# RWKV time mix: four products R k issued ahead of the triangular inversion, the bonus term issued behind the turned blocks

## The chip, the cores and the metric

The kernel runs on one core of a Trainium2 chip. A core has five engines that run their own instruction streams and meet at semaphores: TensorE (PE; its weight loads are listed as PEld), VectorE (DVE), ScalarE (ACT), GpSimd (POOL) and SyncE (SP, which issues transfers). The metric is the device time of one execution, in microseconds (us). Times come from the hardware: medians of timed runs, and one profiled execution whose trace gives every instruction's start and duration.

## The reference

The program is a stack of four layers (each a token mixer and a gated feed-forward block, FFN) on 256 tokens of width 1024, followed by two hybrid attention layers. Layers 0 and 3 mix tokens by RWKV-7. For each of 16 heads of 64 channels it runs, in float32:

```python
def step(state, inp):
    r_t, w_t, k_t, v_t, kk_t, a_t = inp
    sa = jnp.einsum('bhvk,bhk->bhv', state, kk_t)
    state = (state * w_t[:, :, None, :]
             - sa[..., None] * (kk_t * a_t)[:, :, None, :]
             + v_t[..., None] * k_t[:, :, None, :])
    return state, jnp.einsum('bhvk,bhk->bhv', state, r_t)
...
y = ((y - mu) * lax.rsqrt(var + RW_GN_EPS)).reshape(B, S, D) * ln_w + ln_b
y = y + (jnp.sum(rh * kh * r_k, axis=-1, keepdims=True) * vh).reshape(B, S, D)
out = (y * g).astype(h.dtype) @ w_out
```

The second line from the end is the bonus term: for each token and head the sum over channels of r·k·r_k, times the value row.

## The kernel before

Channels lie on partitions, two heads to a tile of 128, so R, K and their kin are eight tiles `c` of 128 x 256 tokens. The recurrence is done in two chunks of 128 tokens. `Rh[:, c]` and `KB[:, c]` hold the scaled r, and the scaled k beside the scaled kk·a. `amat` forms for each head a strictly triangular 128 x 128 matrix (`AKB`), which has to be inverted. The rest of the layer waits for this inversion, which has three parts:

- `inv_diag`: the 32 x 32 blocks on the diagonals of all heads are inverted together on DVE, by 31 steps of two instructions, `tmp` = A times X (L1316) and X += `tmp` (L1318). Each instruction reads what the one ahead of it wrote, so the 62 form one chain. The sizes run from 31 elements per partition up to 256 and down to 31 again.
- `inv_turn`: two DVE transposes of the result, `XN` (L1324) and `XT` (L1326).
- `inv_merge`: PE joins blocks of 32 to 64 and then to 128 (L1346, L1360, L1362, L1370, L1373), and ACT and DVE copy what it makes (L1348, L1351, L1354, L1364, L1366, L1387, L1389). ACT starts with L1351, a copy of `XN`.

Beside the inversion runs work that needs no inverse: for each `c`, `rmat` makes products of R with K and kk·a on PE (L1234), ACT copies them (L1240, into `ark` and over `KB[:, c]`) and POOL cuts triangles out of them (L906). `rmat` also makes `prod` = Rh·KB on DVE (L1237), which must be read before ACT writes over `KB[:, c]`; `rout` sums `prod` over channels on PE (L1246, into the PSUM bank `bo`), and multiplies the triangles with the values (L1252). After tiles 3 and 7, ACT copies the sums to `coef` (L1256). `gtc` is the output gate's product (L1215, L1218 on PE, L1220 on ACT), of which each call fills half. Then `bv` = (Vc + mu)·coef is built in four pieces by two DVE instructions each (L1269, L1271); it is first read in `rwkv_tail` (L1431). `rwkv_tail` holds all that needs the inverse; its first DVE instruction is L1432.

The order on each engine is not that of the source: a scheduler of the tile framework places each engine's instructions by its own estimate, within the dependences and within the buffers that the pools give. `prod` has two buffers, so the third product can't be written before PE has read the first, and so on. An engine executes its list strictly in order, so an instruction that waits holds back all that stand behind it. `tc.issue_after(ins)` keeps what it wraps behind `ins` in the scheduler's list.

Of the kernel before, what the change touches and what calls it, by code (L numbers as in the profile page):

```python
# [9 lines left out]
F32 = mybir.dt.float32  # L10
# [3 lines left out]
ALU = mybir.AluOpType  # L14
# [3 lines left out]
D, S, H, HD, DFF = 1024, 256, 16, 64, 2816  # L18
# [21 lines left out]
class Prog:  # L40
# [502 lines left out]
    def dsa(self, x, i):  # L543
        nc, tc = self.nc, self.tc
        xg, rf = self.prenorm(x, f"norm_mix{i}")
        with tc.tile_pool(name="ds", bufs=1) as sp, tc.tile_pool(name="dsw", bufs=2) as sw:
# [75 lines left out]
            def evac_qk(g, dst, sc):  # L622
                def ev(n, t, ps):
# [4 lines left out]
                    s8 = sw.tile([128, 8], F32, name="s8")  # L628
                    nc.vector.tensor_reduce(s8, sq.rearrange("p (h d) -> p h d", d=64), axis=AX.X, op=ALU.add)
                    rs = self.rstd(s8, scale=1.0 / HD, n=8, load=False)  # L630
# [264 lines left out]
    def rwkv(self, x, i):  # L895
        nc, tc = self.nc, self.tc
# [3 lines left out]
        mm, tt, ts, stt = nc.tensor.matmul, nc.vector.tensor_tensor, nc.vector.tensor_scalar, nc.vector.scalar_tensor_tensor  # L900
# [8 lines left out]
        with ExitStack() as outer:  # L909
# [11 lines left out]
            Vc = sp.tile([128, 2, D], F32, name="Vc")  # L921
# [4 lines left out]
            mu = sp.tile([128, 2, 16], F32, name="mu")  # L926
# [4 lines left out]
            coef = sp.tile([128, 2, 16], F32, name="coef")  # L931
            bcol = sp.tile([128, KT, 4], F32, name="bcol")
            with tc.tile_pool(name="ra", bufs=1) as ra:
# [76 lines left out]
                with tc.issue_after(xv_lo):  # L1010
                    for q, m in ((0, 3), (64, 4)):
                        tt(out=L1m[:, :, q:q + 64], in0=L1.rearrange("p (k n) -> p k n", n=128)[:, :, q:q + 64],
                        in1=C(f"mix{m}", 0, 8)[:, :, None].to_broadcast([128, 8, 64]), op=ALU.mult)
                def evac_v(n, t, ps):
# [16 lines left out]
                    m = mu[:, t, n * 8:n * 8 + 8]  # L1031
                    nc.vector.tensor_reduce(m, v3(v), axis=AX.X, op=ALU.add)
                    ts(m, m, 1.0 / HD, None, op0=ALU.mult)
# [38 lines left out]
            KB = rc.tile([128, KT, 2 * S], F32, name="KB")  # L1072
            Rh = rc.tile([128, KT, S], F32, name="Rh")
# [123 lines left out]
            with ExitStack() as rde:  # L1197
                rd = rde.enter_context(tc.tile_pool(name="rd", bufs=1))
                TT = [rd.tile([128, 16, 128], F32, name="TT0")]
                nc.gpsimd.memset(TT[0], 0.0)  # L1200
                X = self.inv_diag(rd, AKB)
                rt = rde.enter_context(tc.tile_pool(name="rt", bufs=1, side="right"))
                GT = rt.tile([128, KT, S], F32, name="GT")
                TT.append(rt.tile([128, 16, 128], F32, name="TT1"))
                act(TT[1], self.ones[:, None, :128].to_broadcast([128, 16, 128]), AF.Copy, scale=0.0)
                g2 = self.wraw.tile([128, WCH], F32, name="wraw")
                nc.sync.dma_start(g2[:, :1024], self.a["rw_g2a"][l])
                nc.sync.dma_start(g2[:, 1024:1280], self.a["rw_g2b"][l])

                def gtc(a):  # L1210

                    pg = [self.psum("at")[:, :S] for _ in range(4)]
                    for j in range(4):
                        c = 4 * a + j
                        mm(pg[j], g2[:, c * 128:128 + c * 128], sg1, start=True, stop=False)  # L1215
                    for j in range(4):
                        b = slice(32 * j, 32 * j + 32)
                        mm(pg[j], g2[b, 1024 + a * 128:1152 + a * 128], sg2[b], start=False, stop=True)  # L1218
                    for j in range(4):
                        cp(GT[:, 4 * a + j], pg[j])  # L1220
                rex = ExitStack()
                re = rex.enter_context(tc.tile_pool(name="re", bufs=2))
                bo = self.psum("o")
                ark = [re.tile([128, 4, 128], F32, name=f"ark{j}", bufs=1) for j in range(2)]
                prods = {}

                def rmat(c):
                    ak = ark[c % 2]
                    pe = [q4(self.psum("at")) for _ in range(2)]
                    for y in range(2):  # L1230
                        for ch in range(2):
                            for e in range(2):
                                b = slice(e * 64, e * 64 + 64)
                                mm(pe[e][:, 2 * y + ch], KB[b, c, y * S + ch * 128:y * S + ch * 128 + 128],  # L1234
                                   Rh[b, c, ch * 128:ch * 128 + 128], start=True, stop=True)
                    prods[c] = re.tile([128, S], F32, name="prod")
                    tt(out=prods[c], in0=Rh[:, c], in1=KB[:, c, :S], op=ALU.mult)  # L1237
                    for j, d in enumerate((ak, q4(KB[:, c]))):
                        for e in range(2):
                            cp(d[:, e::2], pe[e][:, 2 * j:2 * j + 2])  # L1240
                        lower(d, 0)

                def rout(c):
                    ak, prod = ark[c % 2], prods[c]
                    for t in range(2):
                        mm(bo[:, t * 16 + 2 * c:t * 16 + 2 * c + 2], prod[:, t * 128:(t + 1) * 128], rkb[:, c],  # L1246
                           start=True, stop=True)
                    py = self.psum("mm")[:, :S].rearrange("p (a b) -> p a b", b=64)
                    for ch in range(2):
                        for e in range(2):  # L1250
                            hh = 2 * c + e
                            mm(py[:, 2 * ch + e], ak[:, 2 * ch + e], Vc[:, ch, hh * 64:hh * 64 + 64], start=True, stop=True)  # L1252
                    cp(csT[:, c, :S], py.rearrange("p a b -> p (a b)"))
                    if c % 4 == 3:
                        o = slice(2 * c - 6, 2 * c + 2)
                        cp(coef[:, :, o], bo[:, :32].rearrange("p (a b) -> p a b", a=2)[:, :, o])  # L1256
                    prods[c] = None
                rph = [lambda: rmat(0)] + sum(([lambda c=c: rmat(c + 1), lambda c=c: rout(c)] if c + 1 < KT else [lambda c=c: rout(c)]
                                              for c in range(KT)), [])
                for j, f in enumerate(rph):  # L1260
                    f()
                    if j == 8:
                        gtc(0)
                rex.close()
                bv = rde.enter_context(tc.tile_pool(name="rv", bufs=1)).tile([128, 2, 4, 2, 2, 64], F32, name="bv")
                for q in range(2):
                    for ch in range(2):
                        bc = lambda u: u[:, ch, 8 * q:8 * q + 8].rearrange("p (c e) -> p c e", e=2)[:, :, :, None].to_broadcast([128, 4, 2, 64])
                        tt(out=bv[:, q, :, ch], in0=Vc[:, ch, 512 * q:512 * q + 512].rearrange("p (c e v) -> p c e v", e=2, v=64),  # L1269
                           in1=bc(mu), op=ALU.add)  # L1270
                        tt(out=bv[:, q, :, ch], in0=bv[:, q, :, ch], in1=bc(coef), op=ALU.mult)  # L1271
                scr = aT.rearrange("p c t -> p (c t)")
                XNT = self.inv_turn(rd, X)
                og, gts = [None] * KT, [lambda: gtc(1)]
                sc = [scr[:, 1024 * q:1024 * q + 1024] for q in range(2)]
                self.inv_merge([u.rearrange("p a h t -> p (a h) t") for u in AKB], XNT, TT, sc, lambda: gts and gts.pop()())

                def chain(q):
                    return self.rwkv_tail(q, rc, rt, l, Vc, AKB[q], KB, TT[q], csT, Rh, N0, W00, WK1, scol, bv[:, q], GT, sc[q], C, og)
                add = lambda c, ps: self.new_x(c, x[c], ps)  # L1280
                A, B, i, rest = chain(0), chain(1), 0, []
                while A or B:
                    if A and next(A, 1):
                        A = None
                        rest = self.ohalf(self.a["rw_out"][l], 0, og, add)
                    if B and i >= RLAG and next(B, 1):
                        B = None
                    for f in rest[:RFO]:
                        f()
                    rest = rest[RFO:]  # L1290
                    i += 1
                for f in rest + self.ohalf(self.a["rw_out"][l], 1, og, add):
                    f()
# [27 lines left out]
    def inv_turn(self, rd, X):  # L1321
        nc = self.nc
        XN = rd.tile([128, 32, 32], F32, name="XN_", tag="i1")
        nc.vector.transpose(XN, X.rearrange("p i j -> p j i"))  # L1324
        XT = rd.tile([128, 32, 32], F32, name="XT_", tag="i0")
        nc.vector.transpose(XT.rearrange("p a b -> p (a b)"), X.rearrange("p a b -> p (a b)"))  # L1326
        return XN, XT, rd.tile([128, 32, 32], F32, name="M1", tag="i2")

    def inv_merge(self, AKBs, XNT, TTs, scrs, turn):
# [369 lines left out]
```

## Time and profile before

| | |
|---|---|
| median of 3 runs | 1827.63 us (1822.09 to 1831.22) |
| profiled execution | 1820.38 us, of which the span of the trace is 1818.6 us |
| busy in the span | PE 95%, DVE 75%, ACT 56%, POOL 2% |
| mean granted PE clock | 0.963 of 2.4 GHz |
| `inv_diag`'s chain, first RWKV layer | first L1316 at 146.28 us, XN (L1324) at 185.19 us |
| the same, second RWKV layer | 1220.43 us and 1259.81 us |

Times within the trace count from the span's start. The profiled execution is 7.25 us (0.4%) below the median and 1.7 us below the fastest of the timed runs, so a sum made on the trace is made against 1820.38 us and then carried over to the median. A busy share is an average over stages; what a change is worth is read in its stage.

### The profile page before, as it was taken

To read this page: it belongs to the slowest core of one execution; us is meant where nothing else is said; L and a number is where in the kernel's file an instruction comes from. 1 tells how busy PE (TensorE), PEld (TensorE's weight loads), DVE (VectorE), ACT (ScalarE), POOL (GpSimd) and SP (SyncE) were. 2 spreads that over 40 slices of the span, in tenths; PEclk is the share of its full clock that TensorE was granted. 3 is DMA by queue.
4 is the path that set the end of the run, shared out by engine and by line. 5 is a ranking of instruction groups with operands and counts; after the bars stand their busy time and mean duration, and the time that the engine had idled before them with its cause. 6 is when DMAs were issued, how large, how long until landed. Compare 5 with 4: busy or idle time off the path is not lost.

```text
span 1818.6 us, 34203 instructions
## 1 busy us (share of the span) xinstructions
PE 1730.9 (95%) x13780; PEld 1571.9 (86%) x13780; DVE 1364.0 (75%) x2691; ACT 1021.4 (56%) x1851; POOL 36.4 (2%) x78
## 2 busy tenths in 40 slices
PE   7997899999999999999999989897999998999998
PEld 5696889999899999877999977786999997886876
DVE  8887499866688876799887669787686656676666
ACT  4965355555676455557645445764364445665664
POOL 0003000000000000000000000011000000000000
PEclk9997699999999999999999999986999999999999
DMA  6331048746427855633585542321155455433440
GB/s 218 111 108 47 14 169 302 249 162 225 162 96 280 290 191 176 234 124 116 202 312 207 175 155 101 121 86 44 31 214 187 162 185 206 163 140 124 175 161 24
DMA packets 53451, 293.23 MB, mean 161 GB/s; under 512 B 6651, under 2 KB 9739, under 8 KB 28588
## 3 DMA queue, kind: packets, MB, share of 16 engines
q1 hardware_dynamic: 49148, 285.66, 43.8%
q10 hardware_dynamic: 4144, 5.39, 0.9%
q8 instruction: 108, 1.77, 0.4%
q14 instruction: 51, 0.42, 0.1%
HBM read 288.92 MB, written 2.11 MB: 160 GB/s over the span
## 4 chain that ended last, share of the span: by engine, by line
PE 73%; DVE 14%; DMA 6%; ACT 4%; issue 3%; ACTq 0%; SPq 0%; DVEq 0%; POOLq 0%
PE mm L114 14%; PE mm L116 13%; PE mm L115 13%; PE mm L219 6%; PE mm L220 5%; PE mm L221 5%; DMA adaw<-ada 4%; DVE wlo L108 4%; DVE junk L675 1%; ACT whi L107 1%; PE o L508 1%; PE at L472 1%; PE at L1153 1%; PE at L1234 1%; PE at L495 1%
## 5 line engine op out<-in xcount | busy, mean ns | idle before, releaser
L108 DVE TENSOR_TENSOR wlo<-wraw,whi 128x1024 fp32r<-128x1024 f32 (+2 forms) x518 | 588.5, 1140 | 229.7 <-ACT whi L107 227.6
L107 ACT CAST whi<-wraw 128x1024 fp32r<-128x1024 f32 (+2 forms) x518 | 504.4, 983 | 312.2 <-PE mm L116 181.8
L1527 ACT ACTIVATE sg<-gt 128x256 f32<-128x256 f32 x88 | 36.8, 418 | 84.8 <-DVE gt L1524 84.7
L219 PE MATMUL mm<-whi,xgh 128*128 128x512 f32 x192 | 79.9, 419 | 3.3 <-ACT xgh L734 3.3
L220 PE MATMUL mm<-wlo,xgh 128*128 128x512 f32 x192 | 76.1, 397 | 0.1
L221 PE MATMUL mm<-whi,xgl 128*128 128x512 f32 x192 | 75.9, 398 | 0.0
L114 PE MATMUL mm<-mh,whi 128*128 128x256 f32 x256 | 73.9, 289 | 1.1 <-ACT sg L1062 0.6
L115 PE MATMUL mm<-mh,wlo 128*128 128x256 f32 x256 | 71.7, 280 | 0.0
L116 PE MATMUL mm<-ml,whi 128*128 128x256 f32 x256 | 71.6, 280 | 0.0
L1524 DVE TENSOR_TENSOR gt<-mm,rr 128x512 f32<-128x512 f32 x88 | 60.5, 688 | 12.7 <-PE mm L116 11.6
L675 DVE SCALAR_TENSOR_TENSOR junk<-adaw,cs 128x1024 f32<-128x1024 f32 x48 | 58.6, 1222 | 14.5 <-DMA adaw<-ada 14.1
L115 PE MATMUL mm<-xg0h,wlo 128*128 128x256 f32 x192 | 54.1, 282 | 4.6 <-DVE wlo L108 4.6
L114 PE MATMUL mm<-xg0h,whi 128*128 128x256 f32 x192 | 54.9, 286 | 0.8 <-ACT whi L107 0.8
L116 PE MATMUL mm<-xg7l,whi 128*128 128x256 f32 x192 | 53.5, 279 | 0.5 <-DVE xg7l L132 0.5
L114 PE MATMUL mm<-xg4h,whi 128*128 128x256 f32 x192 | 53.7, 280 | 0.0
L116 PE MATMUL mm<-xg0l,whi 128*128 128x256 f32 x192 | 53.3, 278 | 0.0
L114 PE MATMUL mm<-xg1h,whi 128*128 128x256 f32 x192 | 53.3, 278 | 0.0
L115 PE MATMUL mm<-xg1h,wlo 128*128 128x256 f32 x192 | 53.3, 277 | 0.0
L114 PE MATMUL mm<-xg5h,whi 128*128 128x256 f32 x192 | 53.3, 277 | 0.0
L116 PE MATMUL mm<-xg4l,whi 128*128 128x256 f32 x192 | 53.3, 277 | 0.0
L115 PE MATMUL mm<-xg5h,wlo 128*128 128x256 f32 x192 | 53.3, 277 | 0.0
L115 PE MATMUL mm<-xg4h,wlo 128*128 128x256 f32 x192 | 53.3, 277 | 0.0
(825 smaller groups left out, 6009.8 us busy)
## 6 DMA issues: line engine op xcount, KB each, us to landing
wraw<-ffn_gu SPq DMA_DIRECT2D x88, 1024.0 KB, 5.0
wraw<-ffn_dn SPq DMA_DIRECT2D x64, 704.0 KB, 4.0
adaw<-ada SPq DMA_DIRECT2D x48, 512.0 KB, 5.1
wraw<-hy_qkv SPq DMA_DIRECT2D x24, 1024.0 KB, 4.9
wraw<-rw_k SPq DMA_DIRECT2D x8, 1024.0 KB, 4.9
wraw<-rw_r SPq DMA_DIRECT2D x8, 1024.0 KB, 4.9
wraw<-rw_out SPq DMA_DIRECT2D x8, 1024.0 KB, 4.8
wraw<-sb_qk SPq DMA_DIRECT2D x8, 1024.0 KB, 4.7
```

Of the source, the lines that this page charges most:

```text
L107: nc.scalar.copy(hi, rw)
L108: nc.vector.tensor_tensor(out=lo, in0=rw, in1=hi.bitcast(F32), op=ALU.subtract)
L114: mm(ps, w[0], x[0], start=first, stop=False, **kw)
L115: mm(ps, w[1], x[0], start=False, stop=False, **kw)
L116: mm(ps, w[0], x[1], start=False, stop=last, **kw)
L219: mm(ps, x[0], w[0], start=first, stop=False)
L220: mm(ps, x[0], w[1], start=False, stop=False)
L221: mm(ps, x[1], w[0], start=False, stop=last)
L472: nc.tensor.matmul(z[e][:, o:o + n], qT[b, hp, t * 128:t * 128 + 128], kT[b, hp, :n], start=True, stop=True)
L675: nc.vector.scalar_tensor_tensor(out=junk, in0=raw, scalar=1.0, in1=self.cs, op0=ALU.mult, op1=ALU.mult, accum_out=self.mod[l][:, j:j + 1])
L1524: nc.vector.tensor_tensor(out=gt, in0=ps.rearrange("p (a b) -> p a b", a=2), in1=r[:, None, :].to_broadcast([128, 2, S]), op=ALU.mult)
L1527: nc.scalar.activation(sg, gt[:, 0], AF.Silu)
```

## The change

`prod` gets four buffers instead of two, in a pool that is opened ahead of `inv_diag`, and the products of tiles 0 to 3 are written ahead of `inv_diag` in the source; those of tiles 4 to 7 stay in `rmat`. The eight instructions of `bv` move from ahead of `inv_turn` to behind `inv_merge` in the source, wrapped so that the scheduler places none of them ahead of `XT`, the second transpose.

```diff
                 nc.gpsimd.memset(TT[0], 0.0)
+                rex = ExitStack()
+                re = rex.enter_context(tc.tile_pool(name="re", bufs=1))
+                prods = []
+
+                def product(c):
+                    prods.append(re.tile([128, S], F32, name="prod", bufs=4))
+                    tt(out=prods[c], in0=Rh[:, c], in1=KB[:, c, :S], op=ALU.mult)
+                for c in range(4):
+                    product(c)
                 X = self.inv_diag(rd, AKB)
...
-                rex = ExitStack()
-                re = rex.enter_context(tc.tile_pool(name="re", bufs=2))
                 bo = self.psum("o")
...
-                    prods[c] = re.tile([128, S], F32, name="prod")
-                    tt(out=prods[c], in0=Rh[:, c], in1=KB[:, c, :S], op=ALU.mult)
+                    if c >= 4:
+                        product(c)
...
                 rex.close()
-                bv = rde.enter_context(tc.tile_pool(name="rv", bufs=1)).tile([128, 2, 4, 2, 2, 64], F32, name="bv")
-                for q in range(2):
-                    for ch in range(2):
-                        bc = lambda u: ...
-                        tt(out=bv[:, q, :, ch], in0=Vc[...], in1=bc(mu), op=ALU.add)
-                        tt(out=bv[:, q, :, ch], in0=bv[:, q, :, ch], in1=bc(coef), op=ALU.mult)
...
                 self.inv_merge([u.rearrange("p a h t -> p (a h) t") for u in AKB], XNT, TT, sc, lambda: gts and gts.pop()())
+                bv = rde.enter_context(tc.tile_pool(name="rv", bufs=1)).tile([128, 2, 4, 2, 2, 64], F32, name="bv")
+                with tc.issue_after(self.turned):
+                    for q in range(2):
+                        for ch in range(2):
+                            bc = lambda u: ...
+                            tt(out=bv[:, q, :, ch], in0=Vc[...], in1=bc(mu), op=ALU.add)
+                            tt(out=bv[:, q, :, ch], in0=bv[:, q, :, ch], in1=bc(coef), op=ALU.mult)
...
-        nc.vector.transpose(XT.rearrange("p a b -> p (a b)"), X.rearrange("p a b -> p (a b)"))
+        self.turned = nc.vector.transpose(XT.rearrange("p a b -> p (a b)"), X.rearrange("p a b -> p (a b)")).ins
```

In the built programs the lists of PE, ACT, POOL and SP hold the same instructions in the same order. Only DVE's list differs, in the same way in both RWKV layers. Behind the changed lines the line numbers of the new source are 6 higher.

DVE before, in the middle of `inv_diag`'s chain, where the instructions are longest:

```order
L1316 TENSOR_TENSOR tmp__1628<-A__1623,X__1625 128x256
L1237 TENSOR_TENSOR prod<-Rh,KB 128x256
L1318 TENSOR_TENSOR X__1625<-X__1625,tmp__1628 128x16x16
L1316 TENSOR_TENSOR tmp__1628<-A__1623,X__1625 128x255
L1318 TENSOR_TENSOR X__1625<-X__1625,tmp__1628 128x15x17
L1316 TENSOR_TENSOR tmp__1628<-A__1623,X__1625 128x252
L1318 TENSOR_TENSOR X__1625<-X__1625,tmp__1628 128x14x18
L1237 TENSOR_TENSOR prod<-Rh,KB 128x256
L1316 TENSOR_TENSOR tmp__1628<-A__1623,X__1625 128x247
```

DVE of the change, ahead of the inversion, behind the last columns of `amat`:

```order
L1085 TENSOR_TENSOR Rh<-mm,E1r 128x256
L1207 TENSOR_TENSOR prod<-Rh,KB 128x256 x2
L1085 TENSOR_TENSOR Rh<-mm,E1r 128x256
L108 TENSOR_TENSOR wlo<-wraw,whi 128x1024 x2
L1160 COPY_PREDICATED akk_665<-pm,at 128x2x128 x2
```

Two of the eight products have left the chain and stand ahead of it; no product is left in it beyond its first step.

DVE before, later in the chain, the first four of the eight instructions of `bv`:

```order
L1318 TENSOR_TENSOR X__1625<-X__1625,tmp__1628 128x9x23
L1269 TENSOR_TENSOR bv<-Vc,mu 128x4x128
L1316 TENSOR_TENSOR tmp__1628<-A__1623,X__1625 128x192
L1271 TENSOR_TENSOR bv<-bv,coef 128x4x128
L1318 TENSOR_TENSOR X__1625<-X__1625,tmp__1628 128x8x24
L1269 TENSOR_TENSOR bv<-Vc,mu 128x4x128
L1316 TENSOR_TENSOR tmp__1628<-A__1623,X__1625 128x175
L1271 TENSOR_TENSOR bv<-bv,coef 128x4x128
```

DVE of the change, in `inv_merge` (L1372 is before's L1366, L1395 its L1389, L1438 its L1432):

```order
L1360 COPY TT_1706<-XT__1935 32x16x32 x2
L1280 TENSOR_TENSOR bv<-Vc,mu 128x4x128 x2
L1372 COPY TT_1612<-at 32x16x32 x2
L1282 TENSOR_TENSOR bv<-bv,coef 128x4x128
L1372 COPY TT_1706<-at 32x16x32 x2
L1282 TENSOR_TENSOR bv<-bv,coef 128x4x128
L1395 COPY TT_1612<-at 64x8x64
L1280 TENSOR_TENSOR bv<-Vc,mu 128x4x128
L1395 COPY TT_1612<-at 64x8x64
L1395 COPY TT_1706<-at 64x8x64
L1282 TENSOR_TENSOR bv<-bv,coef 128x4x128
L1395 COPY TT_1706<-at 64x8x64
```

Behind these follow one more pair of `bv`, and then the tail's first instruction, L1438. The eight instructions have moved from between the chain's steps to between the copies of what PE makes in the merge.

## Rows read from the trace of the kernel before

**Rows 1.** The page: share of the chain that ended last, by engine.
```profile
PE 73%; DVE 14%; DMA 6%; ACT 4%; issue 3%; ACTq 0%; SPq 0%; DVEq 0%; POOLq 0%
```

**Rows 2.** Waits, 144 to 190, then DVE's, 1214 to 1262: total us, times, longest.
```profile
PE mm L1346 <- DVE XN__1945 L1324: 10.4, 1, 10.4
DVE prod L1237 <- PE o L1246: 3.5, 1, 3.5
...
DVE prod L1237 <- PE o L1246: 3.9, 1, 3.9
```

**Rows 3.** Timeline of DVE, first layer: start, us, instruction [idle before].
```profile
163.02 0.43 DVE L1316 TENSOR_TENSOR tmp__1628<-A__1623,X__1625 128x256 f32<-128x256 f32 x1
166.92 0.43 DVE L1237 TENSOR_TENSOR prod<-Rh,KB 128x256 f32<-128x256 f32 x1 [3.48 <-PE o L1246]
167.26 0.85 DVE L1318 TENSOR_TENSOR X__1625<-X__1625,tmp__1628 128x256 f32<-128x256 f32 x1
...
169.84 0.85 DVE L1318 TENSOR_TENSOR X__1625<-X__1625,tmp__1628 128x252 f32<-128x252 f32 x1
...
171.38 0.40 DVE L1316 TENSOR_TENSOR tmp__1628<-A__1623,X__1625 128x247 f32<-128x247 f32 x1
```

**Rows 4.** The same timeline, where `bv` stands in the chain, and its end.
```profile
175.90 0.38 DVE L1318 TENSOR_TENSOR X__1625<-X__1625,tmp__1628 128x207 f32<-128x207 f32 x1
176.19 0.68 DVE L1269 TENSOR_TENSOR bv<-Vc,mu 128x512 f32<-128x512 f32 x1
176.79 0.35 DVE L1316 TENSOR_TENSOR tmp__1628<-A__1623,X__1625 128x192 f32<-128x192 f32 x1
...
183.04 0.28 DVE L1316 TENSOR_TENSOR tmp__1628<-A__1623,X__1625 128x112 f32<-128x112 f32 x1
...
185.19 1.90 DVE L1324 STREAM_TRANSPOSE XN__1945<-X__1625 128x1024 f32<-128x1024 f32 x1
```

**Rows 5.** The same timeline, the same sizes on the chain's way up.
```profile
152.91 0.30 DVE L1318 TENSOR_TENSOR X__1625<-X__1625,tmp__1628 128x135 f32<-128x135 f32 x1
153.25 0.32 DVE L1316 TENSOR_TENSOR tmp__1628<-A__1623,X__1625 128x156 f32<-128x156 f32 x1
...
155.50 0.37 DVE L1316 TENSOR_TENSOR tmp__1628<-A__1623,X__1625 128x207 f32<-128x207 f32 x1
```

**Rows 6.** Timeline of ACT: the last copy of the gate, first and second layer.
```profile
176.76 1.20 ACT L1220 COPY GT<-at 128x256 f32<-128x256 f32 x4 [1.17 <-PE at L1218]
...
1251.38 1.21 ACT L1220 COPY GT<-at 128x256 f32<-128x256 f32 x4 [1.17 <-PE at L1218]
```

**Rows 7.** Timeline of DVE, second layer: XN, a late copy, the tail's start.
```profile
1259.81 1.90 DVE L1324 STREAM_TRANSPOSE XN__14910<-X__14590 128x1024 f32<-128x1024 f32 x1
...
1282.03 0.68 DVE L1389 COPY TT<-at 64x512 f32<-64x512 f32 x1 [0.25 <-PE at L1373]
...
1286.64 0.69 DVE L1432 TENSOR_TENSOR W<-mm,csT 128x512 f32<-128x512 f32 x1 [3.93 <-PE mm L1420]
```

**Rows 8.** Timeline of DVE ahead of the inversion, first layer.
```profile
128.35 0.42 DVE L1085 TENSOR_TENSOR Rh<-mm,E1r 128x256 f32<-128x256 f32 x1 [2.33 <-PE mm L116]
```

**Rows 9.** Timeline of DVE in the merge and at the tail's start, first layer.
```profile
194.26 1.40 DVE L1366 COPY TT<-at 32x512 f32<-32x512 f32 x2 [2.72 <-PE at L1362]
197.50 1.40 DVE L1366 COPY TT<-at 32x512 f32<-32x512 f32 x2 [1.85 <-PE at L1362]
...
205.85 0.68 DVE L1389 COPY TT<-at 64x512 f32<-64x512 f32 x1 [1.02 <-PE at L1373]
...
216.49 0.69 DVE L1432 TENSOR_TENSOR W<-mm,csT 128x512 f32<-128x512 f32 x1 [6.54 <-PE mm L1420]
```

**Rows 10.** Stretches: busy us of each engine, PE clock, DMA share, GB/s.
```profile
163.00:166.00 3.00, 2.56 (x26) 1.72 (x25) 0.43 (x1) 1.21 (x4) 0.00 (x0) 0.92 0.00 0
...
214.00:217.00 3.00, 3.00 (x26) 3.00 (x25) 0.51 (x1) 0.59 (x1) 0.00 (x0) 0.89 0.00 0
...
1277.00:1280.00 3.00, 3.00 (x53) 3.00 (x51) 0.68 (x1) 0.58 (x1) 0.00 (x0) 0.56 0.04 5
```

More of the change, by code (lines that the diff above doesn't have):

```diff
@@ L1220, in gtc @@
                         cp(GT[:, 4 * a + j], pg[j])
-                rex = ExitStack()
-                re = rex.enter_context(tc.tile_pool(name="re", bufs=2))
                 bo = self.psum("o")
                 ark = [re.tile([128, 4, 128], F32, name=f"ark{j}", bufs=1) for j in range(2)]
-                prods = {}
                 def rmat(c):
@@ L1256, in rout @@
                         cp(coef[:, :, o], bo[:, :32].rearrange("p (a b) -> p a b", a=2)[:, :, o])
-                    prods[c] = None
                 rph = [lambda: rmat(0)] + sum(([lambda c=c: rmat(c + 1), lambda c=c: rout(c)] if c + 1 < KT else [lambda c=c: rout(c)]
@@ L1264, in rwkv @@
                 rex.close()
-                bv = rde.enter_context(tc.tile_pool(name="rv", bufs=1)).tile([128, 2, 4, 2, 2, 64], F32, name="bv")
-                for q in range(2):
-                    for ch in range(2):
-                        bc = lambda u: u[:, ch, 8 * q:8 * q + 8].rearrange("p (c e) -> p c e", e=2)[:, :, :, None].to_broadcast([128, 4, 2, 64])
-                        tt(out=bv[:, q, :, ch], in0=Vc[:, ch, 512 * q:512 * q + 512].rearrange("p (c e v) -> p c e v", e=2, v=64),
-                           in1=bc(mu), op=ALU.add)
-                        tt(out=bv[:, q, :, ch], in0=bv[:, q, :, ch], in1=bc(coef), op=ALU.mult)
                 scr = aT.rearrange("p c t -> p (c t)")
@@ L1276, in rwkv @@
                 self.inv_merge([u.rearrange("p a h t -> p (a h) t") for u in AKB], XNT, TT, sc, lambda: gts and gts.pop()())
+                bv = rde.enter_context(tc.tile_pool(name="rv", bufs=1)).tile([128, 2, 4, 2, 2, 64], F32, name="bv")
+                with tc.issue_after(self.turned):
+                    for q in range(2):
+                        for ch in range(2):
+                            bc = lambda u: u[:, ch, 8 * q:8 * q + 8].rearrange("p (c e) -> p c e", e=2)[:, :, :, None].to_broadcast([128, 4, 2, 64])
+                            tt(out=bv[:, q, :, ch], in0=Vc[:, ch, 512 * q:512 * q + 512].rearrange("p (c e v) -> p c e v", e=2, v=64),
+                               in1=bc(mu), op=ALU.add)
+                            tt(out=bv[:, q, :, ch], in0=bv[:, q, :, ch], in1=bc(coef), op=ALU.mult)
                 def chain(q):
```

## The prediction

> **What bounds the kernel now.** I read the page first, then the waits, then the timeline of one RWKV layer engine by engine. The chain that ended last lies on PE for 73% and on DVE for 14% [rows 1], so over the whole program PE is the bound. A few microseconds on DVE count only where PE stands and waits for DVE. The waits say where that is: in front of L1346, the merge's first product, PE idles 10.4 us, and what ends it is the transpose XN [rows 2]. XN stands at the end of `inv_diag`'s chain, so in this stretch the DVE chain is the path, and whatever lies between its steps delays everything behind it. The reader should see two such things. One is a product that DVE reaches at 163.45 and can't start before 166.92, because PE has not yet read the buffer that it wants [rows 3]; DVE executes in order, so X, which is ready, stands behind it. The other is `bv` [rows 4], which nothing reads before the tail.
>
> **What the change does, term by term, in the first RWKV layer.** Only DVE's list changes.
>
> 1. The product that stalls. `tmp` ends at 163.02 + 0.43 = 163.45, X starts at 167.26 [rows 3]. Without the product X starts some 0.03 behind `tmp`, at 163.48. That is 3.78 us: the wait of 3.48 and the start-to-start time of the product.
> 2. The second product. X of size 252 ends at 169.84 + 0.85 = 170.69, so `tmp` could start at 170.72; it starts at 171.38 [rows 3]. That is 0.66 us.
> 3. `bv`. X of size 207 starts at 175.90 and lasts 0.38; its successor could start at 176.31. Eight steps and eight `bv` instructions later the step of size 112 starts at 183.04 [rows 4]. The same eight sizes on the way up show what the steps need alone: 2.25 us for those of 156, 175 and 192 (153.25 to 155.50) and 0.34 for each of 135 (152.91 to 153.25), so 2.25 + 0.68 = 2.93 [rows 5]. Without `bv` the step of size 112 starts at 176.31 + 2.93 = 179.24, which is 3.80 us sooner.
>
> The Trainium skill (VectorE: DVE Perf Modes, section "The DRAIN you can't avoid") says that a DVE instruction doesn't start before the pipeline is empty, and that a semaphore between two costs nothing extra. By that, each `bv` would give back its whole duration. The rows disagree: `bv` occupies 0.60 from its start to the next (176.19 to 176.79), and the steps beside it become cheaper, since something independent covers their waits. Term 3 would be eight times 0.68 = 5.4 us by the durations; I take 3.80, by the rows.
>
> The sum is 3.78 + 0.66 + 3.80 = 8.24 us: XN starts at 185.19 - 8.24 = 176.95 and ends 1.90 later, at 178.85. In the second layer the wait is 3.9 instead of 3.5 [rows 2], the rest I take as equal: 8.7 us.
>
> What could hide behind it: ACT copies XN first thing in the merge, and PE multiplies it. ACT is done with its earlier work at 176.76 + 1.20 = 177.96, after PE's last gate product, so XN still comes last, by 0.89 us. In the second layer XN would end at 1259.81 - 8.7 + 1.90 = 1253.0 and ACT is done at 1251.38 + 1.21 = 1252.59 [rows 6, 7]: 0.4 us. The margins are thin, but both engines are free in time, so I let the full sum through.
>
> What the edits add. Two products now stand ahead of the inversion between two instructions L1085, of which the second waits 2.33 us for the projection on PE [rows 8]; that wait hides the two, 0.4 us each, so they cost nothing, and without it at most 0.8 a layer. No instruction of the new list waits for a product's buffer, since PE reads the first four before the inversion starts. The moved `bv` lies in the merge, where DVE waits for PE. Two instructions (about 1.3 us) stand in front of the first L1366, whose wait is 2.72. One stands in each of the next three waits: that of 1.85, that of some 5 us between the end of the second L1366 at 198.90 and the copy ahead of 205.85, and that of 1.02. Two stand in front of L1432, whose wait is 6.54 [rows 9]. One falls between the last two copies, where the wait in the second layer is only 0.25 [rows 7]; that copy would come some 0.4 us late, for the tail's second half, which starts later than its first. The bounds are zero, if the waits cover all, and eight times 0.60 = 4.8 us a layer, if they cover nothing. I take zero, since each wait but one is longer than what now stands in it. Below zero I see nothing, because `bv` feeds only the tail.
>
> Both layers: 8.24 + 8.7 = 16.9 us. Against the profiled execution that is 1820.4 - 16.9 = 1803.5. The profiled execution is 7.25 us below the median; carried over, 1827.6 - 16.9 = **1811 us** (-0.9%). What a measurement of this kernel can tell from no change is about 0.5%, 9.1 us.
>
> **The rivals.**
>
> *The clock moves with the work.* Behind its idle time PE runs the merge at 1.2 GHz. In the first layer the clock comes back to 2.4 within 214 to 217 (0.89 in the mean), while PE runs the tail's first products, in the second at the end of 1277 to 1280 (0.56), still in the merge [rows 10]. From XN to L1432 the first layer takes 216.49 - 185.19 = 31.30 us and the second 1286.64 - 1259.81 = 26.83 [rows 4, 7, 9]. So the place of the rise is worth 4.5 us a layer, and shifting the merge by 8 us can move it either way. If the first layer gets the early rise, 1806.5 by the median; if the second loses it, 1815. The Trainium skill (TensorE: Matmul & The Clock Gate, Part 1) holds that the clock is low by default, that activity releases it, and that the transition varies from run to run; the two layers, which run the same instructions, agree. I expect it to spread the runs of both kernels, not to shift their medians: 1 in 4 that it adds or takes a full 4.5 us net.
>
> *PE and ACT take DVE's place.* The products beside the inversion run at the low clock until the beginning of 163 to 166 (0.92 in the mean) [rows 10]. If the clock came back later there, ACT's last copy of the gate would pass 178.85 and the merge would wait for it. A delay of 4 us would eat the margin of 0.89 and give back 3.1 us a layer, 6 in all: 1817. Against it: the old stall hung on the same products, so when they are late the kernel before loses too. 7 in 100.
>
> *The first layer's gain is lost in the FFN behind it,* because transfers pace that: then only 8.7 us remain, 1819. Against it: in the tail the transfers stand still (share 0.00 in 214 to 217, [rows 10]), so they wait for the work and start sooner with it. 5 in 100.
>
> *Slower.* The merge starts sooner and the clock stays low through the tail. PE is busy there throughout (3.00 of 3 us, [rows 10]), so a rise that comes d us later costs up to d/2. The gain of both layers is gone when the rise is 17 us late in each (in the first layer at 231.6 instead of 214.7); at 26 us in each the time is 1827.6 - 16.9 + 26 = 1837, half a per cent above before. No row shows a rise that late. 3 in 100.
>
> **How the numbers follow.** The forecast, with the clock's 4.5 us either way, has 85 in 100 and lies at 1806 to 1816 by itself; the scatter of the timed runs (1822 to 1831) adds some 3 us to a median. The range of **1802 to 1820** holds the second and third rivals too. Faster by over 0.5% means below 1818.5: the forecast, most of the second rival, and none of the third: 0.85. Within 0.5%: 0.12. Slower: 0.03.
>
> **What would show it.** In the profile after, DVE has no wait for L1246 inside the chain, and the chain runs without a gap between steps from size 112 on; XN starts near 177 in the first layer; PE's idle time in front of L1346 (then L1352) falls from 10.4 us to about 2; from XN to the tail's first DVE instruction it takes between 26.8 and 31.3 us as before. Term 2 is wrong if the products ahead of the inversion delay it; the cost of zero for `bv` is wrong if PE waits for a DVE copy in the merge by more than before. The prediction fails if ACT or PE is found to start the merge late, or if the FFN behind the first layer begins sooner and ends no sooner.

## The result, and the profile after

| | before | after |
|---|---|---|
| median | 1829.01 us (1822.09 to 1831.22, 4 runs) | 1802.32 us (1796.62 to 1807.28, 4 runs) |
| ratio, 95% interval | | 0.9869 [0.9842, 0.9896] |
| profiled execution | 1820.38 us | 1799.19 us (span 1797.5) |

By the ratio the kernel is 24 us faster, by the two medians 26.7, where the forecast was 16.9. The page first: the share of each engine in the chain that ended last.

```profile
PE 72%; DVE 15%; DMA 5%; ACT 4%; issue 2%; ACTq 0%; SPq 0%; DVEq 0%; POOLq 0%
```

As before [rows 1], PE is the bound of the program. The waits of the first RWKV layer (144 to 215): total us, times, longest.

```profile
PE mm L1352 <- DVE XN__1933 L1330: 2.8, 1, 2.8
ACT aT L1357 <- DVE XN__1933 L1330: 1.5, 1, 1.5
```

PE's idle time ahead of the merge has fallen from 10.4 us [rows 2] to 2.8, DVE has no wait for the sums of products any more, and ACT still waits for XN, so XN still comes last. The timeline of DVE in that layer: two of the products ahead of the inversion; the place where the kernel before stalled [rows 3]; the part of the chain where `bv` stood [rows 4]; XN, and `bv` among the merge's copies [rows 9].

```profile
126.02 0.74 DVE L1207 TENSOR_TENSOR prod<-Rh,KB 128x256 f32<-128x256 f32 x2
128.43 0.42 DVE L1085 TENSOR_TENSOR Rh<-mm,E1r 128x256 f32<-128x256 f32 x1 [1.67 <-PE mm L116]
...
163.15 0.42 DVE L1322 TENSOR_TENSOR tmp__1639<-A__1634,X__1636 128x256 f32<-128x256 f32 x1
163.61 0.42 DVE L1324 TENSOR_TENSOR X__1636<-X__1636,tmp__1639 128x256 f32<-128x256 f32 x1
...
171.19 0.38 DVE L1324 TENSOR_TENSOR X__1636<-X__1636,tmp__1639 128x207 f32<-128x207 f32 x1
171.59 0.36 DVE L1322 TENSOR_TENSOR tmp__1639<-A__1634,X__1636 128x192 f32<-128x192 f32 x1
...
177.28 1.91 DVE L1330 STREAM_TRANSPOSE XN__1933<-X__1636 128x1024 f32<-128x1024 f32 x1
...
183.66 1.29 DVE L1280 TENSOR_TENSOR bv<-Vc,mu 128x512 f32<-128x512 f32 x2
186.34 1.40 DVE L1372 COPY TT<-at 32x512 f32<-32x512 f32 x2 [1.39 <-PE at L1368]
187.67 0.67 DVE L1282 TENSOR_TENSOR bv<-bv,coef 128x512 f32<-128x512 f32 x1
189.58 1.40 DVE L1372 COPY TT<-at 32x512 f32<-32x512 f32 x2 [1.24 <-PE at L1368]
...
208.79 0.69 DVE L1438 TENSOR_TENSOR W<-mm,csT 128x512 f32<-128x512 f32 x1 [5.44 <-PE mm L1426]
```

The products fill a part of the wait of 2.33, of which 1.67 is left; the chain runs without a gap where the stall was; XN starts at 177.28 instead of 185.19. In the merge DVE still waits ahead of each copy. From XN's start to the tail's first DVE instruction (L1438, before L1432; below it is called the tail's first addition) it takes 31.5 us. In the second layer, from the same view, it takes 1271.97 - 1244.85 = 27.1:

```profile
1244.85 1.92 DVE L1330 STREAM_TRANSPOSE XN__14898<-X__14601 128x1024 f32<-128x1024 f32 x1
...
1266.43 0.68 DVE L1395 COPY TT<-at 64x512 f32<-64x512 f32 x1 [0.25 <-PE at L1379]
1267.04 0.67 DVE L1282 TENSOR_TENSOR bv<-bv,coef 128x512 f32<-128x512 f32 x1
1267.64 0.68 DVE L1395 COPY TT<-at 64x512 f32<-64x512 f32 x1
...
1271.97 0.69 DVE L1438 TENSOR_TENSOR W<-mm,csT 128x512 f32<-128x512 f32 x1 [2.33 <-PE mm L1426]
```

The difference of 4.4 us is the clock's. Two windows of each layer, which lie between 17 and 26 us behind XN (busy time of the engines, then the granted clock of PE, where 1.00 is 2.4 GHz and 0.50 is 1.2):

```profile
194.00:197.00 3.00, 3.00 (x48) 3.00 (x48) 0.78 (x2) 0.58 (x1) 0.00 (x0) 0.50 0.00 0
200.00:203.00 3.00, 3.00 (x22) 2.88 (x20) 2.54 (x5) 0.00 (x0) 0.00 (x0) 0.50 0.28 93
...
1265.00:1268.00 3.00, 3.00 (x45) 2.93 (x42) 2.32 (x5) 0.58 (x1) 0.00 (x0) 0.94 0.30 99
1268.00:1271.00 3.00, 3.00 (x30) 3.00 (x29) 1.61 (x3) 1.17 (x2) 0.00 (x0) 1.00 0.20 71
```

The same matmuls there, by line, in the first layer and then in the second (busy us, mean ns of one):

```profile
L1379 PE MATMUL at<-TT,aT 64*64 64x64 f32 x64 | 7.1, 312 | 0.0
L1417 PE MATMUL mm<-W,TT 128*128 128x64 f32 x16 | 3.7, 424 | 0.0
...
L1379 PE MATMUL at<-TT,aT 64*64 64x64 f32 x64 | 5.5, 266 | 0.0
L1417 PE MATMUL mm<-W,TT 128*128 128x64 f32 x16 | 2.0, 278 | 0.0
```

So the clock rises either "early", about 20 us behind XN, while PE still runs L1379, or "late", at 29 us or more, and then the tail's first addition comes 4.4 us later; these two groups alone make up 3.3 of it. The two layers of the kernel before show the same two cases [rows 9, 7].

### The profile page after: what moved, and what is told of

Its sections match the earlier page's. It is cut to its first block, busy times and chain, and to the rows that moved or that the text cites. A ratio compares the mean times of both kernels' runs of the same rounds, so it can differ in the third digit from the quotient of the medians.

```text
span 1797.5 us, 34205 instructions
## 1 busy us (share of the span) xinstructions
PE 1724.3 (96%) x13780; PEld 1566.6 (87%) x13780; DVE 1364.6 (76%) x2691; ACT 1019.8 (57%) x1851; POOL 35.7 (2%) x78
## 4 chain that ended last, share of the span: by engine, by line
PE 72%; DVE 15%; DMA 5%; ACT 4%; issue 2%; ACTq 0%; SPq 0%; DVEq 0%; POOLq 0%
PE mm L114 14%; PE mm L115 14%; PE mm L116 14%; PE mm L219 6%; PE mm L220 5%; PE mm L221 5%; DVE wlo L108 4%; DMA adaw<-ada 4%; DVE junk L675 1%; ACT whi L107 1%; PE o L508 1%; PE at L472 1%; PE at L1153 1%; PE at L495 1%; PE mm L1426 1%
## 5 line engine op out<-in xcount | busy, mean ns | idle before, releaser
L108 DVE TENSOR_TENSOR wlo<-wraw,whi 128x1024 fp32r<-128x1024 f32 (+2 forms) x518 | 588.2, 1139 | 229.7 <-ACT whi L107 227.9
L675 DVE SCALAR_TENSOR_TENSOR junk<-adaw,cs 128x1024 f32<-128x1024 f32 x48 | 58.5, 1220 | 15.1 <-DMA adaw<-ada 15.0
```

Of the source, the lines that this page charges most:

```text
L108: nc.vector.tensor_tensor(out=lo, in0=rw, in1=hi.bitcast(F32), op=ALU.subtract)
L675: nc.vector.scalar_tensor_tensor(out=junk, in0=raw, scalar=1.0, in1=self.cs, op0=ALU.mult, op1=ALU.mult, accum_out=self.mod[l][:, j:j + 1])
```

## The experiments

Times at the head of each are the median, the ratio to the kernel before with its interval, and the number of runs. The ratio is taken against runs of the kernel before that belong to the same experiment; it differs from the quotient of the two medians by up to 0.3%. "Chain" is below the time from the transpose ahead of `inv_diag` to XN; "place" is XN's start less the last rise of the granted clock ahead of it, by the trace's record of the clock. Both are given for the first and the second RWKV layer of the profiled execution.

### Both kernels again

The first two were run right behind the result. The last two came later; the "place theory" that they name is the subject of the section on XN's place.

`e1_after_again`, 1806.3 us, 0.9877 [0.9833, 0.9921], 6 runs.

> The changed kernel once more, timed in more rounds. Theory (the terms of the sum): the change is worth 16 to 17 us, so the ratio comes out near 0.991 and the 95% interval takes in 0.991; the chain from the DVE transpose A to XN is 7.9 to 8.7 us shorter than before in each RWKV layer again, and whatever lies beyond that in the profile sits in the dense matmul stages, where the start-to-start time of the 128x256 matmuls is either 113 or 118 ns, in other stages than in the first profile. Rival (something beyond the two RWKV stretches is gained): the ratio stays at 0.987 or below, and the same stages are again shorter than before by more than a microsecond.

`e2_before_again`, 1825.61 us, one run.

> The kernel before once more, one look. Theory: the time of one execution scatters by up to 10 us with the code unchanged, because the dense matmul stages run at 113 or at 118 ns per 128x256 matmul (in the first profile of before the last FFN of 180 us ran at 118). So in this profile the pattern of fast and slow stages differs from the first one, while the RWKV chain from A to XN is the same to 1 us. Rival: the pattern belongs to the code; then the same stages are slow again (the last FFN at 118 ns).

`e10_after_third`, 1802.96 us, one run.

> The changed kernel once more, one look. Place theory: in both layers XN starts 13.3 to 14.4 us behind the clock's last rise; up to 14.0 it takes 27 us from XN to the first addition, at 14.4 and above 31 us or more. Luck: no such order.

`e11_before_third`, 1828.86 us, one run.

> The kernel before once more, one look. Place theory: in both layers XN starts 21.1 to 22.1 us behind the clock's last rise; from 21.5 on it takes 31 us or more from XN to the first addition, at 21.1 or less 27 us. Luck: no such order.

With the two profiles shown, each kernel gives six layers:

| | chain | place | XN to the first addition |
|---|---|---|---|
| before | 40.47, 40.93; 40.15, 40.67; 40.55, 40.59 | 21.7, 21.1; 22.1, 21.5; 21.6, 21.6 | 31.3, 26.8; 32.8, 31.4; 31.3, 31.4 |
| after | 32.43, 32.34; 32.28, 32.30; 32.28, 32.36 | 14.4, 13.6; 14.0, 13.3; 13.8, 13.6 | 31.5, 27.1; 27.0, 27.3; 27.1, 27.1 |

The chain is 8.23 us shorter in the mean (40.56 to 32.33). XN to the first addition falls by 2.98 us in the mean (30.83 to 27.85), because the kernel before rose late in five layers of six and the changed one in one of six. From there to the last tile of `og`, the layer's gated output, it is 35.7 us in all twelve but one (37.2). Summed over all of it and both layers: 22.9 us, and the two comparisons measured 0.9873 in the mean, 23.2 us of 1825. So chain and clock together account for the gain, as closely as the intervals can tell (some 5 and 8 us to either side). The same sum for the kernels below, against the kernel before, lies within 5.4 us of what their ratios say (sum, then ratio, in us: `e3` -10.6 and -12.8, `e4` -16.0 and -12.0, `e5` -1.7 and 0, `e12` +10.9 and +11.7, `e6` -22.0 and -16.6, `e7` -11.6 and -13.0, `e8` -15.0 and -13.5, `e9` -18.6 and -15.1).

Of the expectations, the chain came out as `e1_after_again` had it, but its ratio of 0.991 did not: the ratio stayed near its rival's, and what comes on top of the chain lies in the merges, not in the dense stages. The two rates of the dense stages did change places from run to run, as `e2_before_again` had it (last section). All four layers of the last two runs rose as their places said.

### One half of the change at a time

`e3_products_only`: the first four pieces of the diff, `bv` where it was. 1810.48 us, 0.993 [0.9893, 0.9967], 10 runs. Chain 39.20 and 39.18.

```
+                for c in range(4):
+                    product(c)
                 X = self.inv_diag(rd, AKB)
...
                 rex.close()
                 bv = rde.enter_context(tc.tile_pool(name="rv", bufs=1)).tile([128, 2, 4, 2, 2, 64], F32, name="bv")
```

> Only the first half of the change: four buffers and the products ahead; the bonus term stays in the chain. Theory: terms 1 and 2 alone, 3.78 + 0.66 = 4.4 us in the first layer and about 4.8 in the second, 9.2 us in all, a ratio near 0.995; no wait of DVE for L1246's kind in the chain. Rival (the wait only moves: DVE comes to the bonus term before ACT has copied the sums it needs): a new wait in front of one of the bonus instructions of 1 us or more, and less than 3.5 us a layer gained.

`e4_bv_only`: the products as before, `bv` behind the turned blocks. 1810.58 us, 0.9934 [0.9906, 0.9961], 12 runs. Chain 36.78 and 36.87.

```
-                bv = rde.enter_context(tc.tile_pool(name="rv", bufs=1)).tile([128, 2, 4, 2, 2, 64], F32, name="bv")
...
                 self.inv_merge([u.rearrange("p a h t -> p (a h) t") for u in AKB], XNT, TT, sc, lambda: gts and gts.pop()())
+                bv = rde.enter_context(tc.tile_pool(name="rv", bufs=1)).tile([128, 2, 4, 2, 2, 64], F32, name="bv")
+                with tc.issue_after(self.turned):
```

> Only the second half of the change: the bonus term behind the transposes; the products keep two buffers. Theory: term 3 alone, 3.8 us a layer, 7.6 us in all, ratio near 0.996; the wait for the product's buffer stays at 3.5 to 4 us. Rival (by the durations of the eight instructions): 5.4 us a layer, 10.9 in all. Second rival (the merge pays for them): the stretch from XN to the tail's first DVE instruction is longer by up to 4.8 us a layer and nothing is gained.

`bv` alone shortens the chain by 3.7 us (40.56 to 36.83), the products alone by 1.4 us (to 39.19), and both by 8.2. The products' half is short by 3.1 us for a reason that DVE's timeline and PE's of `e3_products_only` show:

```profile
177.48 0.69 DVE L1274 TENSOR_TENSOR bv<-Vc,mu 128x512 f32<-128x512 f32 x1 [3.52 <-PE mm L1258]
...
176.37 1.00 PE L1258 MATMUL mm<-Vc,ark 128*128 128x64 f32 x8
```

Without the stall the chain reaches the first `bv` sooner, and `bv` can't start: it waits 3.52 us for PE's last L1258 (before's L1252), which reads `ark` until 177.37. By the code, `bv`'s pool is opened where the pool of `ark` and the products has been closed, so it can get their space; that this is the reason was not tried by itself. In `e4_bv_only` the old stall is still there:

```profile
DVE prod L1237 <- PE o L1246: 3.6, 1, 3.6
```

So the products are worth 1.4 us a layer while `bv` stands in the chain, and 4.5 without it. For `e3_products_only` the rival was right that a new wait would eat the gain, though it named another one (for ACT's copies). That its time lies near the 9.2 us of the theory (12.8 by the ratio) is luck: by the profile the chain gives 2.7 us over both layers, and early rises of the clock give 7.3. In `e4_bv_only` the chain gave the 3.8 us of the theory, not the 5.4 of the rival, and the merge didn't pay for `bv`: XN to the first addition took 26.8 and 26.9 us. Its time too owes as much to early rises (8.0 us over both layers) as to the chain (7.5).

### Does XN's place decide the merge's clock?

In the layers so far, the clock rose early up to a place of 14.0, late at 14.4, early at 17.6 to 21.1 (the two halves are at 20.4 and 17.6 to 17.8, and all four of their layers took 26.8 to 27.2) and late from 21.5. The length of PE's pause ahead of the merge doesn't sort them: it is 10.4 us in all six layers of the kernel before, of which one rose early and five late. To tell the place from luck, XN is moved without touching anything else: idle instructions on DVE between the chain and XN.

```
+        for _ in range(2):
+            nc.vector.tensor_tensor(out=X, in0=X, in1=X, op=ALU.max)
         nc.vector.transpose(XN, X.rearrange("p i j -> p j i"))
```

`e5_pad_before`: the kernel before with two. 1826.08 us, 1.000 [0.9974, 1.0027], 12 runs.

> The kernel before, with two idle DVE instructions (X = max(X, X), 128x1024, about 1.2 us each by the split L108 of that size) between the chain's end and the transpose XN, in both layers. Work is added on the path that I found to set the end, so by the sums of durations alone (rival: the late clock rises of the merge are luck of a run) it costs 2 x 2.4 = 4.8 us, ratio 1.0026, and from XN to the tail's first addition it takes 27 us in some layers and 31 in others, as in the four layers seen of the kernel before (31.3, 26.8, 32.8, 31.4; mean 30.6). Theory 'place': what decides between 27 and 31 us is how long after PE's last clock rise XN starts, and the stall of L1207 held the kernel before at 21.1 to 22.1 us, where three of four layers rose late. The padding moves XN to 23.5 to 24.5 us behind that rise, out of that place. Then XN to the first addition is 27 us in nearly all layers, and the padding costs nothing or less: 2 x (2.4 - 3.6) = -2.4 us, ratio 0.996 to 1.000. If both layers show 31 us there, the place theory holds for the two places only and tells nothing of a third.

`e12_pad3_before`: with three. 1837.54 us, 1.0064 [1.0038, 1.0091], 12 runs.

> The kernel before with three idle instructions (about 3.7 us) instead of two ahead of XN. Two cost nothing (ratio 1.0), since both layers then rose early. Sum of durations alone, taken from there: one more costs 2 x 1.24 = 2.5 us (1826 to 1828). Place: XN moves from 23.5 to about 24.7 to 25.5 us behind the clock's last rise. The places seen alternate, early up to 14.0, late at 14.4 to 15.2, early at 16.1 to 21.1, late at 21.5 to 22.1, early at 23.5 to 23.7, so just behind an early place a late one follows: XN to the first addition 31 us or more in both layers, and the third idle instruction costs 2 x (1.24 + 4) = 10.5 us (about 1836, ratio 1.005). If both layers are early again, the order of places can't be carried on beyond what was seen.

DVE's timeline in the second layer, with two idle instructions and then with three (the last of them shown):

```profile
1257.93 2.48 DVE L1325 TENSOR_TENSOR X__14592<-X__14592 128x1024 f32<-128x1024 f32 x2
1260.45 1.90 DVE L1326 STREAM_TRANSPOSE XN__14912<-X__14592 128x1024 f32<-128x1024 f32 x1
...
1287.76 0.69 DVE L1434 TENSOR_TENSOR W<-mm,csT 128x512 f32<-128x512 f32 x1 [3.92 <-PE mm L1422]
```

```profile
1279.59 1.23 DVE L1325 TENSOR_TENSOR X__14593<-X__14593 128x1024 f32<-128x1024 f32 x1
1280.85 1.91 DVE L1326 STREAM_TRANSPOSE XN__14913<-X__14593 128x1024 f32<-128x1024 f32 x1
...
1312.22 0.69 DVE L1434 TENSOR_TENSOR W<-mm,csT 128x512 f32<-128x512 f32 x1 [6.61 <-PE mm L1422]
```

With two, places 23.7 and 23.5, it takes 27.2 and 27.3 us from XN on: a chain 3 us longer in each layer (43.45 and 43.61), and no time lost. With three, places 25.7 and 25.0, it takes 32.8 and 31.4, and the third instruction, 1.24 us long, costs 11.5 us over both layers by the medians (11.7 by the ratios). Durations can't explain that; the place can, and the expectations named the early rises of the first and the late ones of the second ahead.

`e6_pad1_after`: the changed kernel with one. 1811.19 us, 0.9909 [0.9882, 0.9937], 12 runs.

> The changed kernel with one such idle instruction (1.2 us) ahead of XN in both layers. Luck: it costs 2 x 1.2 = 2.4 us against the changed kernel (about 1807, ratio to before about 0.989), and XN to the first addition stays at 27 us in three layers of four. Place: in the changed kernel XN starts 13.3 to 14.4 us behind the clock's rise; at 13.3, 13.6 and 14.0 the merge rose early, at 14.4 late. With 1.2 us more XN stands at 14.5 to 15.6 and both layers rise late: XN to the first addition 31 us, so 1.2 + 3.2 = 4.4 us a layer, 9 us in all (about 1813, ratio about 0.993).

`e7_pad2_after`: with two. 1812.81 us, 0.9929 [0.99, 0.9958], 12 runs.

> The changed kernel with two idle instructions (2.4 us) ahead of XN in both layers. Luck: 4.9 us more than the changed kernel, twice what one costs. Place: XN stands 15.7 to 16.8 us behind the rise, between the late 14.4 and the early 17.6 to 17.8 of the kernel with the bonus term alone; if it is early there, the second idle instruction makes the kernel faster than the first alone by 2 x (3.2 - 1.2) = 4 us (about 1809, ratio 0.991), with 27 us from XN to the first addition in both layers; if it is late, 31 us in both and about 1815.

Here the place theory missed where XN would come to stand, and held for what follows from it. With one, both layers lie at 14.0 and took 27.0; I had expected 14.5 to 15.6, but the rise ahead came later in the chain in that execution. With two, the first lies at 16.1 and took 27.6, the second at 15.2 and took 32.8. The times can't tell the two kernels apart. By the ratios the one instruction costs 6.6 us against the changed kernel, by the profile 0.9; whether other runs stood at late places can't be seen, as one was profiled.

Over all layers but those of `e9_warm`, in which PE has other work ahead of XN:

| place, us behind the rise | layers | XN to the first addition |
|---|---|---|
| 9.8 to 11.6 (`e8_split_late`, below) | 2 | 32.8 to 33.2 |
| 13.3 to 14.0 | 7 | 27.0 to 27.3 |
| 14.4 to 15.2 | 2 | 31.5 to 32.8 |
| 16.1 to 21.1 | 6 | 26.8 to 27.6 |
| 21.5 to 22.1 | 5 | 31.3 to 32.8 |
| 23.5 to 23.7 | 2 | 27.2 to 27.3 |
| 25.0 to 25.7 | 2 | 31.4 to 32.8 |

No layer falls out of this order. The bounds of the bands are read off these layers, so they fit by construction; eight of the 26, those of `e5_pad_before`, `e10_after_third`, `e11_before_third` and `e12_pad3_before`, had their rise named ahead. In all 26 the clock falls again 17.1 us behind the rise ahead of XN (in the changed kernel's first layer it rises at 162.84 and falls at 179.91), wherever XN stands. Why early and late places alternate, no run shows.

### A shorter chain still

`e8_split_late`: within the chain DVE also takes one split of the output weights (L108, 1.23 us, with a wait of 0.87 for ACT). It goes behind the turned blocks. 1809.81 us, 0.9926 [0.9895, 0.9957], 10 runs. Chain 30.13 and 30.15.

```
-                st["w"] = self.wload(src[2 * kh + c // 4], 2048)
+                st["w"] = self.wload(src[2 * kh + c // 4], 2048, after=((), (self.turned,) if kh == 0 and c else ()))
```

> The changed kernel with the one split of rw_out's weights that DVE takes within the chain (L108, 1.23 us, and a wait of 0.87 for ACT's copy, rows 150.51) issued behind the turned blocks too. By durations the chain ends 2.0 to 2.1 us earlier in each layer: from the transpose of L1308 to XN 30.3 instead of 32.3 us, and ACT, which in the changed kernel ended its copies 0.8 to 1.5 us before XN did, gets 1.04 us of work less, so it still comes in time or just after. Luck: 2 x 2.0 = 4 us faster than the changed kernel, ratio to before about 0.985. Place: XN then stands 11.3 to 12.4 us behind the rise, where no layer was seen; if it is a late place, each layer gives back 3.5 us and the kernel is 3 us slower than the changed one, with 31 us from XN to the first addition in both layers.

```profile
175.46 1.95 DVE L1330 STREAM_TRANSPOSE XN__1933<-X__1636 128x1024 f32<-128x1024 f32 x1
...
208.65 0.69 DVE L1438 TENSOR_TENSOR W<-mm,csT 128x512 f32<-128x512 f32 x1 [5.71 <-PE mm L1426]
```

The chain is 2.2 us shorter, as expected, and the kernel is not faster than the changed one; by the ratios (0.9926 against 0.9873) it is some 10 us slower, though the intervals touch. XN to the first addition takes 33.2 and 32.8 us. Two things stand behind that: both layers rise late (36 and 31 us behind XN), and ACT's last gate copies (L1229) now end 1.0 and 1.9 us after XN does. Neither was removed by itself. ACT's timeline in the first layer, where XN ends at 177.41:

```profile
177.23 1.20 ACT L1229 COPY GT<-at 128x256 f32<-128x256 f32 x4 [1.17 <-PE at L1227]
178.44 1.99 ACT L1357 COPY aT<-XN__1933 32x512 f32<-32x512 f32 x2
```

### Keeping PE busy ahead of XN

`e9_warm`: seven matmuls of ones, whose result nothing reads, behind the gate's last product. 1814.32 us, 0.9917 [0.9887, 0.9948], 6 runs. Chain 32.28 and 32.34.

```
+                def warm():
+                    gtc(1)
+                    for _ in range(7):
+                        mm(wm, self.ones[:, :128], self.ones, start=True, stop=True)
+                og, gts = [None] * KT, [warm]
```

> The changed kernel with seven matmuls of ones (128x256, about 0.4 us each at 2.4 GHz by the L1224 matmuls of that size; their result is used nowhere) that PE does in the gap of 2.8 us in which it waits for XN. Their time is free, as PE waited there. They ask whether PE's pause ahead of XN is what lets the clock fall within the merge (2.6 to 3.8 us after XN starts in the changed kernel). Theory 'the pause lets it fall': the clock stays at 2.4 GHz past the first matmuls of the merge; from XN to the first addition it takes clearly less than the 27 us of an early rise (if the fall comes only 10 us later, about 22), and the kernel is about 10 us faster than the changed one, ratio about 0.982. Rival, 'the merge's small matmuls let it fall': the fall stays where it was, XN to the first addition remains 27 or 31 us by XN's place, and the time is that of the changed kernel (ratio 0.987 to 0.988).

PE's timeline at XN, first layer (each of the seven has two records, hence x14):

```profile
178.19 3.29 PE L1277 MATMUL o<-ones 128*128 128x256 f32 x14
181.41 3.63 PE L1358 MATMUL mm<-XN__1933,AKB 32*32 32x32 f32 x122
```

The windows there, with the clock at 1.00 into the second, and the merge's first matmuls by line:

```profile
177.00:184.00 7.00, 7.00 (x117) 5.68 (x117) 6.81 (x12) 3.92 (x8) 0.00 (x0) 1.00 0.41 153
184.00:190.00 6.00, 6.00 (x184) 6.00 (x180) 3.10 (x6) 5.86 (x8) 0.00 (x0) 0.68 0.01 3
```

```profile
L1358 PE MATMUL mm<-XN__1933,AKB 32*32 32x32 f32 x128 | 3.8, 228 | 0.0
```

For comparison the same matmuls in the first layer of `e5_pad_before`, all of which ran at 1.2 GHz, with a window around them:

```profile
L1348 PE MATMUL mm<-XN__1945,AKB 32*32 32x32 f32 x128 | 3.8, 229 | 12.9 <-DVE XN__1945 L1326 12.9
...
189.00:196.00 7.00, 5.21 (x165) 5.21 (x168) 6.14 (x8) 5.12 (x6) 0.00 (x0) 0.50 0.01 4
```

A miss for both theories. The clock did fall later, 8.2 and 6.0 us behind XN instead of 2.6 to 3.8 (20.5 us behind the rise instead of 17.1), so PE's pause has a part in it. But the matmuls that ran at 2.4 GHz for it, 32 x 32, take 228 ns there and 229 at 1.2 GHz, and the 128 of them 3.8 us in both, so nothing was won. The seven took 3.29 us, more than the pause, and PE began the merge 3.4 us behind XN's start in the first layer instead of 2.0 (in the changed kernel L1352 starts at 179.25). XN to the first addition took 28.5 and 31.7 us, with an early and a late rise, and by the ratios the kernel is some 8 us slower than the changed one.

## Why the prediction was right, and where not

**The bound** was read rightly: XN ended PE's wait, and what the chain lost came out at the layer's end, with the clock's part on top.

**Terms 1 and 2**, 4.44 us: both kernels' chains differ by 8.23, and `bv` alone gives 3.73, so the products give 4.50. They do so only with `bv` out of the chain: alone they gave 1.4. The prediction's sum didn't say that, because it looked at the two halves one beside the other.

**Term 3**, 3.80 us: 3.73 measured in `e4_bv_only`. The 5.4 us by durations did not come: a `bv` instruction of 0.68 us gave back 0.47. The prediction had named them after the Trainium skill (VectorE: DVE Perf Modes, section "The DRAIN you can't avoid"), by which a DVE instruction waits for the one ahead of it to leave the pipeline, and had rightly not taken them; the same section says that an instruction which isn't held starts earlier. The trace fits the latter: 0.60 us lie between the start of a `bv` of 0.68 us and the next start [rows 4].

**The sum** per layer, 8.24 and 8.7: 8.04 and 8.59 in the profiles shown. The measured median of 1802.32 stands 0.3 us inside the range of 1802 to 1820 and 9 us below the forecast of 1811. The range held because it had room for the clock's 4.5 us and for the scatter of the runs, not because of the sum.

**The margins** held: ACT was done 1.5 and 1.1 us before XN ended (0.89 and 0.4 forecast). `e8_split_late` shows that they were the whole of it: 2.2 us more, and ACT comes last.

**The costs of zero** held. The second L1085 still waits for PE. In the merge PE waits for no DVE copy but XN. Where the rise is early, XN to the first addition is 27.0 to 27.6 us with `bv` in the merge and all four products early, and 26.8 to 27.3 in the kernels without one or both of these.

**The step that failed** is the clock: "I expect it to spread the runs of both kernels, not to shift their medians". The sum put the clock at nothing; by the twelve layers it is worth 2.98 us a layer, 6.0 of the 22.9. I had read one early and one late layer in the profile as a fair coin. But the kernel before stands at places from 21.1 to 22.1, of which all but the lowest are late ones, and the changed one at 13.3 to 14.4, of which all but the highest are early ones. The price of 4.5 us for one rise was about right: early layers took 26.8 to 27.6 us, late ones 31.3 to 32.8 (`e8_split_late` left aside). The Trainium skill (TensorE: Matmul & The Clock Gate, Part 1) says that the point of the change depends on where PE's work falls in something free-running, that is, something that the kernel doesn't set. The traces agree as far as they go: in the twelve layers above, the rise ahead of XN comes 18.0 to 19.8 us behind the chain's first transpose, though PE's instructions there are the same.

What stays open: six layers of each kernel are few, so the 2.98 us is uncertain, although the chain's part isn't; and a profile can't say ahead of a run in which place a layer will stand, only which places are near. Why a place is early or late stays open too.

**The rivals.** PE and ACT did not take DVE's place, the first layer's gain was not lost in the FFN (the layers' 22.9 us arrive as 23.2, give or take the intervals), and the slow rival, a rise that comes 17 us later, came about in no run: the latest rises stand 36 us behind XN (`e2_before_again`, `e7_pad2_after`, `e8_split_late`, `e12_pad3_before`), where the first layer of the kernel before had 29.5.

## What to carry to other kernels

Look at what a wait holds back and at what is next in line for the same wait: here an edit that takes 4.5 us from a chain took only 1.4 by itself, because an instruction later in the chain waited for the same engine, and the edit beside it happened to move that one away. Before costing a clock rise as luck, put each layer's start against the last rise and see whether the cases sort; where they do, moving work by a microsecond can cost or give back several, and an idle instruction is the cheapest way to find out. A chain that has become shorter than its neighbour's margin (here ACT's 1 us) can be expected to give nothing more until that neighbour moves too; `e8_split_late` fits that, but its late clock rises hide how much of its loss is ACT's.

## What the runs showed of the hardware

Executions of the same kernel differ by 10 us and more, and a part of it lies in the dense stages, at the full clock. Windows of 40 us in two FFN stages, the kernel before and then `e2_before_again` (PE busy with its number of matmuls, then the granted clock):

```profile
360.00:400.00 40.00, 40.00 (x355) 1.00 0.44 150
1400.00:1440.00 40.00, 40.00 (x342) 1.00 0.50 180
```

```profile
360.00:400.00 40.00, 40.00 (x342) 1.00 0.45 151
1400.00:1440.00 40.00, 40.00 (x355) 1.00 0.54 187
```

PE is busy all the time and the clock is granted in full, but a stage runs at one of two rates, 4% apart (from start to start 113.3 and 117.8 ns in these windows, without a gap between the records), and which of the two a stage has changes from execution to execution of the same program. A single profile pair can carry several microseconds of that either way. What sets the rate was not tried.
